# Down tiles that begin wide, wide, narrow, narrow; r copied out of its bank by ScalarE; w_out begun with four column tiles; four other orders of the gates' triples

## The chip, the cores and the metric

The kernel runs on one core of one Trainium2 chip, as one launch. The metric is the device time of an execution in microseconds (us); the lower the better. Before the change three runs took 1267.32, 1267.71 and 1268.02 us, the median is 1267.71.

## The reference

A decoder trunk of two layers on 256 tokens of width 1024, in float32. A layer is a SwiGLU feed-forward (half a step), token mixers in parallel, and a second SwiGLU. Cut to the lines that matter here (`attention` and `gated_linear` stand for the two mixers, which the change doesn't touch):

```python
for l in range(2):
    x = x + 0.5 * swiglu(rmsnorm(x, ffn1_norm[l]), ffn1_w_gate[l], ffn1_w_up[l], ffn1_w_down[l])
    proj = rmsnorm(x, mix_norm[l]) @ w_in[l]             # 1024 -> 6440
    # q_a, kv_a, g_a, q_b, k_b, v_b, a_lr, r_b, g_merge = the column groups of proj
    o_a = attention(q_a, kv_a, sigmoid(g_a))
    o_b = gated_linear(q_b, k_b, v_b, a_lr)
    o_b = rmsnorm(o_b, gla_out_norm[l]) * silu(r_b)
    gm = sigmoid(g_merge)                                # 2 x 1024 columns
    y = gm[0] * (o_a @ w_branch_nsa[l]) + gm[1] * (o_b @ w_branch_gla[l])
    x = x + y @ w_out[l]
    x = x + 0.5 * swiglu(rmsnorm(x, ffn2_norm[l]), ffn2_w_gate[l], ffn2_w_up[l], ffn2_w_down[l])
return rmsnorm(x, final_norm)
# swiglu(x, g, u, d) = (silu(x @ g) * (x @ u)) @ d, with 2816 hidden columns
```

## The kernel before, in words

**Products.** A float32 operand is split into a high part (a cast to float32r) and the low rest. A product is then three matmuls, high by high, high by low, low by high. `mm3` (L120 to L124) issues the three; each is *narrow* (256 columns) or *wide* (512), depending on what streams. `mm2` (L126 to L130) does it in two: a wide one of the weights' high part against [x high | x low] (512 columns), and a narrow one of the weights' low part against x high (256). A pair leaves its two products in the two halves of a bank of PSUM, which are added later. The matmuls of a pair stand at L129 (wide) and L130 (narrow), those of a triple at L122, L123 and L124.

**Weights.** Every weight is read once. A chunk comes from memory by a DMA on SyncE's queue into one of three raw buffers, ScalarE casts it to the high part (L76), and VectorE subtracts to get the low part (L86). `W.prep()` does half a chunk; its calls are written into the program at fixed places, and `W.take()` does what is still missing of the next chunk. Split chunks lie in three buffers.

**The order of the work** is written out by hand: each engine runs its instructions in the order in which the program issues them, and the engines are held together by semaphores. There is no planner.

**FFN** (`ffn`, four times). 22 column tiles of gate and up (`ff`, pairs) make the hidden values h in 22 k-parts; then 8 down tiles `dn` (j = 0 to 7) are made, each from 22 k in two halves of 11 (one chunk each). Tiles 0 to 6 use pairs, tile 7 uses narrow triples (`mmx`, L346), so that only half a bank has to be added at the end. `add_half` (L353) adds 0.5 of the bank to x in two instructions, or in one for j = 7; w_out uses it too (its factor is taken up by the gate). `post_x` then makes x's high and low parts `xh` and `xl` (`split_x`) and the square for the next norm's sum. In the last FFN, `final_x` transposes finished tiles between two halves.

**Mixer** (`mixer`, twice). First come columns in narrow triples, then `block` (L511) eight times: 512 columns for two groups of 128 tokens (tt), with x standing as the weights operand and 512 weight columns streaming, so wide triples, called A (x high by weight high), B (x high by weight low) and C (x low by weight high) in the change. The blocks are v (2), r (2) and the merge gates (n = 0, 1 by e = 0, 1; `gm`). Each block takes two banks of the pool "mm", which has only two, so the next block waits until the last one's banks are read. `slot()` lets the work of attention and of the gated linear mixer in between the matmuls.

For r, ScalarE makes tanh of the bank (`rth`, L539) and VectorE makes (tanh + 1) * bank (`rt`, L541): it is the last reader of the bank. Between them `W.prep()` puts a weight cast and a split.

Then the merge `mg` (wide triples, three chunks for each e) makes y from two branches; gated sums `ym`, `yn` on VectorE (L563, L622) are transposed by PE (`turn`, L569, into `yt`) and split into high and low (`parts`, L576 on ScalarE, L577 on VectorE).

**w_out** makes 8 column tiles `wo` of pairs over 8 k, two to a chunk; the last tile uses triples. The first 4 k are of y's first half (e = 0) and the last 4 k of its second. The first two tiles run interleaved, with the last token group's transposes between them:

```python
for q in range(2):
    for n in range(2):
        for k in range(4 * q, 4 * q + 4):
            self.mm2(bs[n], wh[:, n * NK + k], wl[:, n * NK + k], y[k], k == 0, k == NK - 1)
        if q == 0:
            turn(u[1], 1, yb, (n,))
            parts(ys[n], yb[n], halves[1])
```

Of the kernel before, what the change touches and what calls it, by code (L numbers as in the profile page):

```python
# [9 lines left out]
AF = mybir.ActivationFunctionType  # L10
OP = mybir.AluOpType
# [6 lines left out]
T = 256  # L18
L = 2
FF = 2816  # L20
NK = D // P
NFF = FF // P
# [79 lines left out]
class Trunk:  # L102
# [29 lines left out]
    def mmt(self, b, x, tt, wh, wl, first, last):  # L132

        s = slice(tt * P, tt * P + P)
        self.mm3(b, x[0][:, s], x[1][:, s], wh, wl, first, last)

    def halves(self, o, b):
        self.nc.scalar.activation(o, b[:, T : 2 * T], AF.Copy)  # L138
# [98 lines left out]
    def ffn(self, l, f, next_gain, hook=None):  # L237
        nc, W = self.nc, self.W
        start = l == 0 and f == 0
        hs = []  # L240
        lows = []

        def gate(i, b):

            u = self.t2(f"u{self.uid()}")
            g = u[:, 0:T]
            self.halves(g, b)
            nc.vector.tensor_mul(g, g, self.rbc)  # L248
            nc.scalar.activation(g, g, AF.Silu)  # L249
            return u  # L250

        def gate2(u):
            nc.vector.tensor_mul(u[:, 0:T], u[:, 0:T], self.rbc)

        def up(i, u, b):
            if i % 2 == 0:
                hs.extend(self.splits("h", 2))
            h = u[:, T : 2 * T]
            self.halves(h, b)
            nc.vector.tensor_mul(h, u[:, 0:T], h)  # L260
            nc.scalar.activation(hs[i][0], h, AF.Copy)  # L261
            lows.append((hs[i][1], h, hs[i][0].bitcast(F32)))

        def low():
            nc.vector.tensor_sub(*lows.pop(0))

        wait = None
        for i in range(NFF):
            wh, wl = W.take()
            bs = [self.bank(f"ff{self.uid()}") for _ in range(2)]  # L270
            if i == 0:
                for k in range(NK):
# [24 lines left out]
            W.prep()  # L297
            if not (i == 1 and start):
                gate2(u)
            for k in range(NK):  # L300
                self.mm2(bs[1], wh[:, NK + k], wl[:, NK + k], self.xx[k], k == 0, k == NK - 1)
            if i == 1 and start:
                self.rstd_row()
                u0 = gate(0, wait[0])
                W.prep()
                gate2(u0)
                up(0, u0, wait[1])
                u = gate(i, bs[0])
                W.prep()
                gate2(u)  # L310
                up(i, u, bs[1])
            else:
                up(i, u, bs[1])
                W.prep()
            low()
            if hook:
                hook(i)
        while lows:
            low()
        for j in range(NK):  # L320
            b = self.bank(f"dn{self.uid()}", "mm")
            for half in range(2):
                wh, wl = W.take()
                for r in range(11):
                    k = half * 11 + r
                    self.mmx(j, b, wh[:, r], wl[:, r], hs[k], k == 0, k == NFF - 1)
                if half == 0 or j < NK - 1:
                    W.prep()
                    W.prep()
                if next_gain is None and half == 0 and j > 0:  # L330
                    self.final_x(j - 1)
                    if j == NK - 1:
# [12 lines left out]

    def mmx(self, j, b, lh, ll, x, first, last):  # L346

        if j < NK - 1:
# [4 lines left out]
    def add_half(self, j, b):  # L353
        for s in (slice(0, T), slice(T, 2 * T))[: 2 if j < NK - 1 else 1]:
            self.nc.vector.scalar_tensor_tensor(self.x[j], b[:, s], 0.5, self.x[j], op0=OP.mult, op1=OP.add)  # L355


    def mixer(self, l, next_gain):
# [149 lines left out]
            for i in range(2):  # L508
                T_pair(lambda ps: scaled(t3[:, 2 * i : 2 * i + 2], ps, c))

        def block(evac):  # L511

            bs = [self.bank(f"mm{self.uid()}", "mm") for _ in range(2)]
            for half in range(2):
                wh, wl = W.take()
                for tt in range(2):
                    rest = None
                    for r in range(4):
                        k = half * 4 + r
                        self.mmt(bs[tt], self.xx[k], tt, wh[:, r], wl[:, r], k == 0, k == NK - 1)  # L520
                        if r == 1:
# [13 lines left out]
        def r_evac(n):  # L535

            def go(tt, b):
                th = self.t2(f"rth{self.uid()}")
                nc.scalar.activation(th, b, AF.Tanh, scale=rs2[:, tt : tt + 1])  # L539
# [9 lines left out]
        gm = []  # L549
        for n in range(2):  # L550
            gm.append([self.t4(f"gm{n}{tt}{l}") for tt in range(2)])
            for e in range(2):
                block(lambda tt, b: nc.scalar.activation(
                    gm[n][tt][:, e * 512 : e * 512 + 512], b, AF.Tanh, scale=rs2[:, tt : tt + 1]) and None)
        while gens:
            slot()

# [23 lines left out]
        for e in range(2):  # L581
# [7 lines left out]
            for c in range(3):  # L589
                wh, wl = W.take()  # L590
                for tt in range(2):
                    b = b1[tt] if c else b0[tt]
                    for r in range(4):
                        x = self.oa[r] if c == 0 else self.ob[4 * c - 4 + r]
                        self.mmt(b, x, tt, wh[:, r], wl[:, r], c < 2 and r == 0, c != 1 and r == 3)
                    if c == 0:
                        gated(0, e, tt, b, u[tt])
                    while pending:
# [27 lines left out]
        wh, wl = W.take()  # L626
        bs = [self.bank(f"wo{self.uid()}", "mm") for _ in range(2)]
        for q in range(2):
            for n in range(2):
                for k in range(4 * q, 4 * q + 4):  # L630
                    self.mm2(bs[n], wh[:, n * NK + k], wl[:, n * NK + k], y[k], k == 0, k == NK - 1)
                if q == 0:
                    turn(u[1], 1, yb, (n,))
                    parts(ys[n], yb[n], halves[1])
                else:
                    self.add_half(n, bs[n])
                    W.prep()
                    self.post_x(n, next_gain[:, n : n + 1])
        for i in range(1, 4):
            wh, wl = W.take()  # L640
            for n in range(2):
                j = 2 * i + n
                b = self.bank(f"wo{self.uid()}", "mm")
                for k in range(NK):
                    self.mmx(j, b, wh[:, n * NK + k], wl[:, n * NK + k], y[k], k == 0, k == NK - 1)
                self.add_half(j, b)
                if j < NK - 1:
                    W.prep()
                self.post_x(j, next_gain[:, j : j + 1])
# [670 lines left out]
```

## Time and profile before

| | us |
|---|---|
| median of three runs | 1267.71 |
| lowest, highest | 1267.32, 1268.02 |
| the profiled execution's own time | 1268.17 |
| its span in the trace | 1266.40 |
| PE, DVE, ACT, POOL busy | 1251.6, 913.9, 711.8, 50.5 |

The mean granted clock of TensorE is 0.998 of full speed, and no slice of the span is lower than nine tenths. The profile is of one execution. PE is TensorE's matmuls, PEld its weight loads, DVE VectorE, ACT ScalarE, POOL GpSimd. In a row of the timeline the first number is the start in us from the span's start, the second the busy time of the instruction (or of the group from its first start to its last end), then engine, line, operation, output and inputs, the size, and how many; in brackets the idle time of the engine before it and what ended that. Matmuls are pipelined, so their busy times overlap, and it is the distance from start to start that tells their pace.

### The profile page before, as it was taken

What the parts mean: (1) busy time and instruction counts of PE and PEld (TensorE: products, weight loads), DVE (VectorE), ACT (ScalarE), POOL (GpSimd) and SP (SyncE); (2) the same over time, 40 slices, a digit from 0 to 9 for tenths busy, and PEclk for the clock granted to TensorE, in tenths of its full rate; (3) what the DMA queues carried; (4) which work ended last, traced back from release to release, by engine and by line L of the source; (5) the groups of instructions that cost most, each with busy time, mean ns of one, the idle gap of its engine ahead of it and who ended that gap; (6) DMA issues with size and microseconds to landing.
All of it is one profiled execution on the core that took longest, in us unless ns stands there. A gap on an engine that the chain in (4) does not pass through costs nothing.

```text
span 1266.4 us, 18985 instructions
## 1 busy us (share of the span) xinstructions
PE 1251.6 (99%) x7396; PEld 1076.0 (85%) x7396; DVE 913.9 (72%) x1690; ACT 711.8 (56%) x1265; POOL 50.5 (4%) x60
## 2 busy tenths in 40 slices
PE   9999999999999999999999999999999999999997
PEld 7888889987778888888888888999777788888886
DVE  6888766774755778886578886567656668888753
ACT  5666545566644556655456664456675445566542
POOL 2001101000010000000010000010000100000000
PEclk9999999999999999999999999999999999999999
DMA  7576767334534445545665546573344354555451
GB/s 272 193 230 211 255 201 264 132 124 137 178 118 144 181 168 205 187 154 198 209 224 208 179 150 205 173 283 135 111 156 164 103 199 148 184 200 185 165 190 59
DMA packets 41001, 227.43 MB, mean 180 GB/s; under 512 B 6949, under 2 KB 8109, under 8 KB 21328
## 3 DMA queue, kind: packets, MB, share of 16 engines
q1 hardware_dynamic: 34352, 213.27, 48.7%
q0 software_dynamic: 5840, 11.87, 2.8%
q8 instruction: 58, 0.95, 0.3%
q10 hardware_dynamic: 720, 1.09, 0.3%
q14 instruction: 31, 0.25, 0.1%
HBM read 225.12 MB, written 2.63 MB: 180 GB/s over the span
## 4 chain that ended last, share of the span: by engine, by line
PE 80%; issue 15%; DVE 2%; ACT 2%; DMA 1%; POOL 0%; POOLq 0%; DVEq 0%; ACTq 0%
PE ff L129 19%; PE ff L130 10%; PE dn L129 9%; PE mm L122 7%; PE mm L123 6%; PE mm L124 6%; PE dn L130 4%; PE wo L129 2%; PE mg L122 2%; PE mg L124 2%; PE mg L123 2%; PE O L150 2%; PE o L150 1%; PE s L150 1%; PE wo L130 1%
## 5 line engine op out<-in xcount | busy, mean ns | idle before, releaser
L76 ACT ACTIVATE wh<-raw 128x1024 fp32r<-128x1024 f32 (+3 forms) x445 | 423.4, 967 | 183.6 <-issue 112.3
L86 DVE TENSOR_TENSOR wl<-raw,wh 128x1024 fp32r<-128x1024 f32 (+3 forms) x445 | 491.3, 1119 | 44.0 <-ACT wh L76 43.7
L129 PE MATMUL ff<-xs,wh 128*128 128x512 f32 x1408 | 489.9, 392 | 0.4 <-DVE xs L162 0.4
L130 PE MATMUL ff<-xs,wl 128*128 128x256 f32 x1408 | 393.9, 280 | 0.7 <-DVE wl L1144 0.5
L129 PEld LDWEIGHTS ff<-xs,wh 128*128 128x128 f32 x1408 | 264.4, 188 | 59.2 <-ACT wh L1143 0.8
L130 PEld LDWEIGHTS ff<-xs,wl 128*128 128x128 f32 x1408 | 264.3, 188 | 1.7 <-DVE wl L1144 1.1
L129 PE MATMUL dn<-h,wh 128*128 128x512 f32 x616 | 218.3, 399 | 0.0
L130 PE MATMUL dn<-h,wl 128*128 128x256 f32 x616 | 173.0, 281 | 0.0
L129 PEld LDWEIGHTS dn<-h,wh 128*128 128x128 f32 x616 | 115.7, 188 | 28.3
L139 DVE TENSOR_TENSOR u<-ff,u 128x256 f32<-128x256 f32 x176 | 74.7, 425 | 60.9 <-ACT u L138 60.9
L130 PEld LDWEIGHTS dn<-h,wl 128*128 128x128 f32 x616 | 116.4, 189 | 0.0
L122 PE MATMUL mm<-wh,xs 128*128 128x512 f32 x256 | 106.2, 415 | 2.5 <-DVE rt L541 2.5
L123 PE MATMUL mm<-wl,xs 128*128 128x512 f32 x256 | 101.5, 396 | 0.0
L124 PE MATMUL mm<-wh,xs 128*128 128x512 f32 x256 | 100.9, 394 | 0.0
L249 ACT ACTIVATE u<-u 128x256 f32<-128x256 f32 x88 | 36.8, 419 | 90.8 <-DVE u L248 90.8
L261 ACT ACTIVATE h<-u 128x256 fp32r<-128x256 f32 x88 | 36.8, 418 | 83.9 <-DVE u L260 83.9
L122 PE MATMUL mm<-xs,wh 128*128 128x256 f32 x256 | 73.8, 288 | 0.0
L124 PE MATMUL mm<-xs,wl 128*128 128x256 f32 x256 | 71.7, 280 | 0.0
L123 PE MATMUL mm<-xs,wh 128*128 128x256 f32 x256 | 71.6, 280 | 0.0
L138 ACT ACTIVATE u<-ff 128x256 f32<-128x256 f32 x176 | 65.6, 373 | 9.8 <-PE ff L130 5.4
L355 DVE SCALAR_TENSOR_TENSOR xs<-dn,xs 128x256 f32<-128x256 f32 x60 | 25.5, 424 | 56.0 <-PE dn L130 38.5
L122 PEld LDWEIGHTS mm<-wh,xs 128*128 128x128 f32 x256 | 48.1, 188 | 19.3 <-issue 4.7
(244 smaller groups left out, 1618.1 us busy)
## 6 DMA issues: line engine op xcount, KB each, us to landing
raw<-in_gu SPq DMA_DIRECT2D x85, 1024.0 KB, 4.9
raw<-in_wd SPq DMA_DIRECT2D x64, 704.0 KB, 4.1
raw<-in_wr SPq DMA_DIRECT2D x32, 1024.0 KB, 4.8
raw<-in_wt SPq DMA_DIRECT2D x16, 1024.0 KB, 5.1
raw<-in_wb SPq DMA_DIRECT2D x12, 1024.0 KB, 4.8
w<-in_w POOLq DMA_DIRECT2D x16, 512.0 KB, 8.6
raw<-in_wo SPq DMA_DIRECT2D x8, 1024.0 KB, 4.9
raw<-in_vg SPq DMA_DIRECT2D x4, 592.0 KB, 3.7
```

The source lines that it names most:

```text
L76: self.nc.scalar.activation(wh[:, s], self.raw[c][:, s], AF.Copy)
L86: self.nc.vector.tensor_sub(wl[:, s], self.raw[c][:, s], wh[:, s].bitcast(F32))
L122: mm(out, lh, rh, start=first, stop=False, skip_group_check=True)
L123: mm(out, lh, rl, start=False, stop=False, skip_group_check=True)
L124: mm(out, ll, rh, start=False, stop=last, skip_group_check=True)
L129: mm(b, lh, x[2], start=first, stop=False, skip_group_check=True)
L130: mm(b[:, 0:T], ll, x[0], start=False, stop=last, skip_group_check=True)
L138: self.nc.scalar.activation(o, b[:, T : 2 * T], AF.Copy)
L139: self.nc.vector.tensor_add(o, b[:, 0:T], o)
L150: self.nc.tensor.matmul(out, l, r, start=first, stop=last, skip_group_check=True)
L249: nc.scalar.activation(g, g, AF.Silu)
L261: nc.scalar.activation(hs[i][0], h, AF.Copy)
```

## The change

1. In a half of a down tile (all but the very last half of j = 7) the first two k go through a new function `mm22`: both wide matmuls first, then both narrow ones.
2. The first half of the last down tile uses pairs like the others, and its second half alone triples; the upper half of the bank is added after the first half. The same for w_out's last tile: its first 4 k are pairs.
3. r: ScalarE does the tanh and then copies the bank to `rt`; VectorE computes in place from the copy.
4. The gates' matmuls of two k at a time are issued in another order: for layer 0 n = 0 "A0 C0 B0 A1 C1 B1", layer 0 n = 1 "C0 A0 B0 C1 A1 B1", layer 1 n = 0 "A0 A1 B0 B1 C0 C1", layer 1 n = 1 "A0 B0 A1 B1 C0 C1". The other users of `mmt` (v, r, merge) keep A0 B0 C0 A1 B1 C1.
5. w_out starts with the first 4 k of three tiles, then all four transposes of the last token group, then the fourth tile's first 4 k, then the second halves of the four tiles. Tiles 0 and 1 lie in banks of the pool "sd", tiles 2 and 3 in "mm". One more half of a weight chunk is prepared in the merge, one less after the first tile.

```diff
+    def mm22(self, b, lh, ll, xs, first):
+        mm = self.nc.tensor.matmul
+        for k in range(2):
+            mm(b, lh[:, k], xs[k][2], start=first and k == 0, stop=False, skip_group_check=True)
+        for k in range(2):
+            mm(b[:, 0:T], ll[:, k], xs[k][0], start=False, stop=False, skip_group_check=True)
...
+    def mmt(self, b, xs, tt, wh, wl, first, last, order="A0 B0 C0 A1 B1 C1"):
         s = slice(tt * P, tt * P + P)
-        self.mm3(b, x[0][:, s], x[1][:, s], wh, wl, first, last)
+        ops = order.split()
+        for n, (o, k) in enumerate(ops):
+            k = int(k)
+            self.nc.tensor.matmul(b, xs[k][1 if o == "C" else 0][:, s], wl[:, k] if o == "B" else wh[:, k],
+                                  start=first and n == 0, stop=last and n == len(ops) - 1, skip_group_check=True)
...
                 wh, wl = W.take()
-                for r in range(11):
+                last = j == NK - 1 and half == 1
+                if not last:
+                    self.mm22(b, wh[:, 0:2], wl[:, 0:2], hs[11 * half : 11 * half + 2], half == 0)
+                for r in range(0 if last else 2, 11):
                     k = half * 11 + r
-                    self.mmx(j, b, wh[:, r], wl[:, r], hs[k], k == 0, k == NFF - 1)
+                    self.mmx(last, b, wh[:, r], wl[:, r], hs[k], False, k == NFF - 1)
...
+                if j == NK - 1 and half == 0:
+                    self.add_half(j, b, (1,))
-            self.add_half(j, b)
+            self.add_half(j, b, (0,) if j == NK - 1 else (1, 0))
...
                 nc.scalar.activation(th, b, AF.Tanh, scale=rs2[:, tt : tt + 1])
-                o = rt[tt][:, n * 512 : n * 512 + 512]
-                return lambda: nc.vector.scalar_tensor_tensor(o, th, 1.0, b, op0=OP.add, op1=OP.mult)
+                nc.scalar.activation(o, b, AF.Copy)
+                return lambda: nc.vector.scalar_tensor_tensor(o, th, 1.0, o, op0=OP.add, op1=OP.mult)
...
+                    (("A0 C0 B0 A1 C1 B1", "A0 A1 B0 B1 C0 C1"), ("C0 A0 B0 C1 A1 B1", "A0 B0 A1 B1 C0 C1"))[l][n])
...
                     W.prep()
+                    if e == 1 and c == 0 and tt == 1:
+                        W.prep()
...
+        ws = [W.take() for _ in range(2)]
+        bs = [self.bank(f"wo{self.uid()}", "sd" if j < 2 else "mm") for j in range(4)]
...
+        for j in range(4):
+            out(j, range(4))
+            if j == 2:
+                turn(u[1], 1, yb)
+                for q in range(2):
+                    parts(ys[q], yb[q], halves[1])
+        for j in range(4):
+            out(j, range(4, NK))
+            self.add_half(j, bs[j])
+            if j:
+                W.prep()
+            self.post_x(j, next_gain[:, j : j + 1])
+        for i in range(2, 4):
```

**Where the instructions move: ScalarE at the end of r, layer 0.** `rth` is the tanh of a bank `mm`, `wh` a weight cast, `gc`, `ga` and `ge` are side work of the gated linear mixer, `gm` the first gate. Before:

```order
L539 ACTIVATE rth_3370<-mm_3310,rs_112_2100 128x512
L76 ACTIVATE wh_3345<-raw_3254 128x1024
L774 ACTIVATE gc_3334<-gb_3263 128x512
L775 ACTIVATE ga_3262<-gb_3263 128x512
L780 ACTIVATE ge_3335<-ge_3335 128x512
L539 ACTIVATE rth_3394<-mm_3311,rs_112_2100 128x512
L76 ACTIVATE wh_3396<-raw_3305 128x1024 x2
```

After:

```order
L560 ACTIVATE rth_3362<-mm_3302,rs_112_2090 128x512
L561 ACTIVATE rt_2402<-mm_3302 128x512
L76 ACTIVATE wh_3337<-raw_3244 128x1024
L808 ACTIVATE gc_3326<-gb_3253 128x512
L809 ACTIVATE ga_3252<-gb_3253 128x512
L814 ACTIVATE ge_3327<-ge_3327 128x512
L560 ACTIVATE rth_3387<-mm_3303,rs_112_2090 128x512
L561 ACTIVATE rt_2403<-mm_3303 128x512
L76 ACTIVATE wh_3390<-raw_3297 128x1024 x2
```

A copy of 128x512 stands behind each tanh, ahead of the weight cast; the third and fourth tanh of a layer have two and three such copies in front of them, counting those of the first block. The rest keeps its order.

**VectorE at the start of w_out, layer 0.** `xs<-wo` is the addition of a tile's bank to x (two instructions), `wl` a weight split, `xs_90` to `xs_92` the low parts `xl` of tiles 0 to 2, `sq` the sum of squares, `y<-yt` the split of y. Before:

```order
L86 TENSOR_TENSOR wl_4050<-raw_3969,wh_4049 128x1024
L577 TENSOR_TENSOR y_3979<-yt_4067,y_3979 128x2x128
L577 TENSOR_TENSOR y_3980<-yt_4068,y_3980 128x2x128
L355 SCALAR_TENSOR_TENSOR xs<-wo_4103,xs 128x256 x2
L86 TENSOR_TENSOR wl_4098<-raw_4021,wh_4097 128x1024
L162 SCALAR_TENSOR_TENSOR xs_90<-xs,sm,xs_90 128x256
L355 SCALAR_TENSOR_TENSOR xs<-wo_4104,xs 128x256 x2
L86 TENSOR_TENSOR wl_4098<-raw_4021,wh_4097 128x1024
L162 SCALAR_TENSOR_TENSOR xs_91<-xs,sm,xs_91 128x256
L175 TENSOR_TENSOR sq_4143<-sq_4143,sq_4163 128x256
L355 SCALAR_TENSOR_TENSOR xs<-wo_4166,xs 128x256 x2
```

After:

```order
L86 TENSOR_TENSOR wl_4068<-raw_4015,wh_4067 128x1024
L599 TENSOR_TENSOR y_3973<-yt_4063,y_3973 128x2x128
L599 TENSOR_TENSOR y_3974<-yt_4064,y_3974 128x2x128
L375 SCALAR_TENSOR_TENSOR xs<-wo_4099,xs 128x256 x2
L175 SCALAR_TENSOR_TENSOR xs_90<-xs,sm,xs_90 128x256
L375 SCALAR_TENSOR_TENSOR xs<-wo_4100,xs 128x256 x2
L86 TENSOR_TENSOR wl_4068<-raw_4015,wh_4067 128x1024
L175 SCALAR_TENSOR_TENSOR xs_91<-xs,sm,xs_91 128x256
L188 TENSOR_TENSOR sq_4155<-sq_4155,sq_4175 128x256
L375 SCALAR_TENSOR_TENSOR xs<-wo_4101,xs 128x256 x2
L86 TENSOR_TENSOR wl_4168<-raw_4035,wh_4167 128x1024
```

The split between the first tile's addition and its `xl` is gone from there; one half chunk is split earlier, in front of the `y` steps (the chunk after the two that w_out's first four tiles use). The third addition, of wo_4101 (j = 2), now frees a bank that the fifth tile takes.

**PE at the start of a down tile.** `h` are two k of the hidden values, each row one matmul of one k. Before:

```order
L129 MATMUL dn_1423<-h_12_304,wh_1300 128x512
L130 MATMUL dn_1423<-h_12_304,wl_1301 128x256
L129 MATMUL dn_1423<-h_12_304,wh_1300 128x512
L130 MATMUL dn_1423<-h_12_304,wl_1301 128x256
L129 MATMUL dn_1423<-h_17_368,wh_1300 128x512
```

After (a row with x2 is two matmuls in a row):

```order
L136 MATMUL dn84_1423<-h0_12_304,wh22_1300 128x512 x2
L138 MATMUL dn84_1423<-h0_12_304,wl22_1301 128x256 x2
L129 MATMUL dn84_1423<-h0_17_368,wh22_1300 128x512
L130 MATMUL dn84_1423<-h0_17_368,wl22_1301 128x256
L129 MATMUL dn84_1423<-h0_17_368,wh22_1300 128x512
```

The second wide matmul has moved ahead of the first narrow one; from the third k on nothing moves.

## Rows read from the trace of the kernel before

**Rows 1.** The page's first part: busy time, share of the span and instructions of each engine.

```profile
span 1266.4 us, 18985 instructions
PE 1251.6 (99%) x7396; PEld 1076.0 (85%) x7396; DVE 913.9 (72%) x1690; ACT 711.8 (56%) x1265; POOL 50.5 (4%) x60
```

**Rows 2.** The waits of PE: engine, line and tile that waited, what it waited for, then us in total, times, longest.

```profile
PE mm L122 <- DVE rt L541: 2.5, 2, 1.2
...
PE yt L569 <- DVE ym L622: 0.8, 2, 0.4
...
PE wo L129 <- DVE y L577: 0.4, 2, 0.2
PE ff L130 <- DVE wl L86: 0.2, 1, 0.2
```

**Rows 3.** Timeline of ACT at the end of the r blocks of layer 0, with the row of the next gap.

```profile
325.15 0.67 ACT L539 ACTIVATE rth<-mm,rs 128x512 f32<-128x512 f32 x1
325.72 1.04 ACT L76 ACTIVATE wh<-raw 128x1024 fp32r<-128x1024 f32 x1
...
328.30 0.67 ACT L539 ACTIVATE rth<-mm,rs 128x512 f32<-128x512 f32 x1
328.87 2.00 ACT L76 ACTIVATE wh<-raw 128x1024 fp32r<-128x1024 f32 x2
333.36 1.06 ACT L76 ACTIVATE wh<-raw 128x1024 fp32r<-128x1024 f32 x1 [2.49 <-issue]
```

**Rows 4.** Timeline of PE at the end of r and the start of the first gate block, layer 0: the last matmul on r's first bank and the first one of the gate block there, then around the second bank.

```profile
325.56 0.39 PE L124 MATMUL mm<-wh,xs 128*128 128x512 f32 x1
327.18 0.50 PE L122 MATMUL mm<-wh,xs 128*128 128x512 f32 x1 [1.23 <-DVE rt L541]
...
329.86 0.39 PE L124 MATMUL mm<-wh,xs 128*128 128x512 f32 x1
330.20 0.50 PE L122 MATMUL mm<-wh,xs 128*128 128x512 f32 x1
```

**Rows 5.** Timeline of DVE in the same stretch: the two steps `rt`, and the weight split between them.

```profile
326.44 0.68 DVE L541 SCALAR_TENSOR_TENSOR rt<-rth,mm 128x512 f32<-128x512 f32 x1
...
328.33 1.22 DVE L86 TENSOR_TENSOR wl<-raw,wh 128x1024 fp32r<-128x1024 f32 x1
329.47 0.68 DVE L541 SCALAR_TENSOR_TENSOR rt<-rth,mm 128x512 f32<-128x512 f32 x1
```

**Rows 6.** Timeline of ACT at an unscaled copy of a 128x512 bank (L809), with the instruction behind it.

```profile
342.51 0.60 ACT L809 ACTIVATE kst<-tb 128x512 f32<-128x512 f32 x1 [1.03 <-PE tb L808]
343.00 1.05 ACT L76 ACTIVATE wh<-raw 128x1024 fp32r<-128x1024 f32 x1
```

**Rows 7.** Timeline of PE in a block of the mixer: two rows with one wide triple between them.

```profile
315.06 0.39 PE L124 MATMUL mm<-wh,xs 128*128 128x512 f32 x1
...
315.76 0.39 PE L124 MATMUL mm<-wh,xs 128*128 128x512 f32 x1
```

**Rows 8.** Timeline of PE in w_out of layer 0: its first matmul, the matmuls ahead of and behind the two pairs of transposes, the first matmul of the third tile (431.27), and the first one behind w_out (448.28).

```profile
423.96 0.48 PE L129 MATMUL wo<-y,wh 128*128 128x512 f32 x1
...
425.34 0.28 PE L130 MATMUL wo<-y,wl 128*128 128x256 f32 x1
426.04 0.44 PE L569 MATMUL yt<-cst,ym 128*128 128x128 f32 x2 [0.42 <-DVE ym L622]
...
427.73 0.38 PE L569 MATMUL yt<-cst,ym 128*128 128x128 f32 x2
428.30 0.50 PE L129 MATMUL wo<-y,wh 128*128 128x512 f32 x1 [0.19 <-DVE y L577]
...
431.27 0.40 PE L129 MATMUL wo<-y,wh 128*128 128x512 f32 x1
...
448.28 0.39 PE L129 MATMUL ff<-xs,wh 128*128 128x512 f32 x1
```

**Rows 9.** Timeline of DVE in w_out of layer 0: the last step of `ym`, and the additions of the first three tiles with the split and `xl` of the first.

```profile
426.35 0.43 DVE L622 TENSOR_TENSOR ym<-ym,yn 128x256 f32<-128x256 f32 x1
...
430.05 0.88 DVE L355 SCALAR_TENSOR_TENSOR xs<-wo,xs 128x256 f32<-128x256 f32 x2 [1.07 <-PE wo L130]
...
432.38 0.88 DVE L355 SCALAR_TENSOR_TENSOR xs<-wo,xs 128x256 f32<-128x256 f32 x2
...
435.04 0.88 DVE L355 SCALAR_TENSOR_TENSOR xs<-wo,xs 128x256 f32<-128x256 f32 x2
```

**Rows 10.** Timeline of ACT in the same place: the step `xh` of the first tile.

```profile
430.97 0.51 ACT L161 ACTIVATE xs<-xs,sm 128x256 fp32r<-128x256 f32 x1 [1.49 <-DVE xs L355]
```

**Rows 11.** Timeline of PE in the last down tile of the first FFN: narrow triples.

```profile
194.00 0.28 PE L122 MATMUL dn<-h,wh 128*128 128x256 f32 x1
194.12 0.28 PE L123 MATMUL dn<-h,wh 128*128 128x256 f32 x1
194.24 0.28 PE L124 MATMUL dn<-h,wl 128*128 128x256 f32 x1
194.36 0.28 PE L122 MATMUL dn<-h,wh 128*128 128x256 f32 x1
```

**Rows 12.** Timeline of PE in an earlier down tile of the first FFN: the first row and the row three pairs later.

```profile
150.09 0.40 PE L129 MATMUL dn<-h,wh 128*128 128x512 f32 x1
...
151.15 0.40 PE L129 MATMUL dn<-h,wh 128*128 128x512 f32 x1
```

**Rows 13.** The same in a down tile of the last FFN, behind transposes of `final_x`.

```profile
1214.41 0.39 PE L129 MATMUL dn<-h,wh 128*128 128x512 f32 x1
...
1215.45 0.39 PE L129 MATMUL dn<-h,wh 128*128 128x512 f32 x1
```

**Rows 14.** Timeline of PE in the merge: two rows with one wide triple between them.

```profile
404.28 0.39 PE L122 MATMUL mg<-wh,ob 128*128 128x512 f32 x1
...
404.96 0.39 PE L122 MATMUL mg<-wh,ob 128*128 128x512 f32 x1
```

More of the change, by code (lines that the diff above doesn't have):

```diff
@@ L130, in mm2 @@
         mm(b[:, 0:T], ll, x[0], start=False, stop=last, skip_group_check=True)
-    def mmt(self, b, x, tt, wh, wl, first, last):
-        s = slice(tt * P, tt * P + P)
-        self.mm3(b, x[0][:, s], x[1][:, s], wh, wl, first, last)
+    def mm22(self, b, lh, ll, xs, first):
[5 more added lines that the diff above has]
+    def mmt(self, b, xs, tt, wh, wl, first, last, order="A0 B0 C0 A1 B1 C1"):
+        s = slice(tt * P, tt * P + P)
+        ops = order.split()
[3 more added lines that the diff above has]
+                                  start=first and n == 0, stop=last and n == len(ops) - 1, skip_group_check=True)
     def halves(self, o, b):
@@ L344, in ffn, with mmx @@
         W.prep()
-    def mmx(self, j, b, lh, ll, x, first, last):
-        if j < NK - 1:
+    def mmx(self, tail, b, lh, ll, x, first, last):
+        if not tail:
             self.mm2(b, lh, ll, x, first, last)
@@ L351, in mmx, with add_half @@
             self.mm3(b[:, 0:T], lh, ll, x[0], x[1], first, last)
-    def add_half(self, j, b):
-        for s in (slice(0, T), slice(T, 2 * T))[: 2 if j < NK - 1 else 1]:
+    def add_half(self, j, b, parts=(1, 0)):
+        for p in parts:
+            s = slice(p * T, p * T + T)
             self.nc.vector.scalar_tensor_tensor(self.x[j], b[:, s], 0.5, self.x[j], op0=OP.mult, op1=OP.add)
@@ L509, in mixer, with block @@
                 T_pair(lambda ps: scaled(t3[:, 2 * i : 2 * i + 2], ps, c))
-        def block(evac):
+        def block(evac, order="A0 B0 C0 A1 B1 C1"):
             bs = [self.bank(f"mm{self.uid()}", "mm") for _ in range(2)]
@@ L517, in block @@
                     rest = None
-                    for r in range(4):
+                    for r in (0, 2):
                         k = half * 4 + r
-                        self.mmt(bs[tt], self.xx[k], tt, wh[:, r], wl[:, r], k == 0, k == NK - 1)
-                        if r == 1:
+                        self.mmt(bs[tt], self.xx[k : k + 2], tt, wh[:, r : r + 2], wl[:, r : r + 2], k == 0, k == NK - 2, order)
+                        if r == 0:
                             slot()
@@ L538, in go @@
                 th = self.t2(f"rth{self.uid()}")
+                o = rt[tt][:, n * 512 : n * 512 + 512]
                 nc.scalar.activation(th, b, AF.Tanh, scale=rs2[:, tt : tt + 1])
-                o = rt[tt][:, n * 512 : n * 512 + 512]
-                return lambda: nc.vector.scalar_tensor_tensor(o, th, 1.0, b, op0=OP.add, op1=OP.mult)
+                nc.scalar.activation(o, b, AF.Copy)
+                return lambda: nc.vector.scalar_tensor_tensor(o, th, 1.0, o, op0=OP.add, op1=OP.mult)
             return go
@@ L553, in mixer @@
                 block(lambda tt, b: nc.scalar.activation(
-                    gm[n][tt][:, e * 512 : e * 512 + 512], b, AF.Tanh, scale=rs2[:, tt : tt + 1]) and None)
+                    gm[n][tt][:, e * 512 : e * 512 + 512], b, AF.Tanh, scale=rs2[:, tt : tt + 1]) and None,
+                    (("A0 C0 B0 A1 C1 B1", "A0 A1 B0 B1 C0 C1"), ("C0 A0 B0 C1 A1 B1", "A0 B0 A1 B1 C0 C1"))[l][n])
         while gens:
@@ L592, in mixer @@
                     b = b1[tt] if c else b0[tt]
-                    for r in range(4):
-                        x = self.oa[r] if c == 0 else self.ob[4 * c - 4 + r]
-                        self.mmt(b, x, tt, wh[:, r], wl[:, r], c < 2 and r == 0, c != 1 and r == 3)
+                    xs = self.oa if c == 0 else self.ob[4 * c - 4 : 4 * c]
+                    for r in (0, 2):
+                        self.mmt(b, xs[r : r + 2], tt, wh[:, r : r + 2], wl[:, r : r + 2], c < 2 and r == 0, c != 1 and r == 2)
                     if c == 0:
@@ L623, in mixer, with out @@
                     W.prep()
[L626 to L639, printed above, removed]
+                    if e == 1 and c == 0 and tt == 1:
+                        W.prep()
+        ws = [W.take() for _ in range(2)]
+        bs = [self.bank(f"wo{self.uid()}", "sd" if j < 2 else "mm") for j in range(4)]
+        def out(j, ks):
+            wh, wl = ws[j // 2]
+            for k in ks:
+                r = j % 2 * NK + k
+                self.mm2(bs[j], wh[:, r], wl[:, r], y[k], k == 0, k == NK - 1)
+        for j in range(4):
[11 more added lines that the diff above has]
+        for i in range(2, 4):
             wh, wl = W.take()
@@ L644, in mixer @@
                 for k in range(NK):
-                    self.mmx(j, b, wh[:, n * NK + k], wl[:, n * NK + k], y[k], k == 0, k == NK - 1)
-                self.add_half(j, b)
+                    self.mmx(j == NK - 1 and k > 3, b, wh[:, n * NK + k], wl[:, n * NK + k], y[k], k == 0, k == NK - 1)
+                    if j == NK - 1 and k == 3:
+                        self.add_half(j, b, (1,))
+                self.add_half(j, b, (0,) if j == NK - 1 else (1, 0))
                 if j < NK - 1:
```

## The prediction, made before the changed kernel ran

> **What bounds the kernel now.** I read the share of busy time first, then the waits of TensorE, then the starts of its matmuls in five places, and last the other engines beside the places that the change touches. TensorE (PE) is busy 99% of a span of 1266.40 us [rows 1]. So the time is the sum of the distances between matmul starts, and another engine counts only where PE waits for it. In the two mixers PE waits twice for the r gate's VectorE step (`rt`), twice for `ym` and twice for `y` before w_out [rows 2]; two times is once per layer, so I work out layer 0 and double it.
>
> All sums are made against the profiled execution's own 1268.17 us (1.77 outside the span); it is 0.46 above the median 1267.71 of the three timed runs, so the forecast is moved down by 0.46 at the end. A measurement of this kernel can tell about 0.2%, 2.5 us, from no change.
>
> **r, copied out of its bank.** ScalarE (ACT) now does tanh and copy, and VectorE works from the copy, so that the bank is free after the copy and no longer after VectorE. In the stretch from 325.15 to 330.87 ACT has no gap [rows 3]: whatever is put in moves all that follows, up to the gap of 2.49 at 333.36, which takes it in. PE's last r matmul of the first bank starts at 325.56, its next one at 327.18, where the beat would be 0.23: 1.39 lost; at the second bank 329.86 to 330.20 loses 0.11 [rows 4]. Both are ended by the VectorE step: it starts 326.44 and 329.47 and takes 0.68, so it ends 327.12 and 330.15 [rows 5].
>
> What a copy costs ACT: the only unscaled copy of a 128x512 bank in the trace takes 0.60, and the next instruction starts 0.49 after it [rows 6]; with a scale operand, as the tanh has, the next starts 0.57 after [rows 3]. I take 0.50, by the row that is alike; the ends are 0.49 and 0.69 (nothing overlaps). Two copies (for the first two tanh) precede the third tanh, which starts at 325.15 + 1.00 = 326.15; its copy runs from 326.72 to 327.32. PE gets the first bank at 327.32 in place of 327.12: +0.20. The fourth tanh has three copies before it: 328.30 + 1.50 = 329.80, its copy 330.37 to 330.97: the second bank is late by 0.82 against 330.15. PE, itself 0.20 late, would be there at 330.09 + 0.20, before the bank is free; so the delays don't add, and the larger one stays. **+0.82 per layer, +1.64 in all.** Bounds: with 0.69 per copy and no overlap the fourth pair starts at 328.30 + 3 x 0.69 = 330.37 and ends 0.67 + 0.60 later, 331.64: +1.5 per layer (+3.0); if the waits simply went, -1.50 per layer (-3.0). The weights' casts stand behind the copies: the gates' second chunk has its last split at 328.33 to 329.55 [rows 5], would have it by about 331, and PE comes to it 8 triples of 0.70 [rows 7] after 327.18, at 332.8. That distance hides it; without it the excess would be seen in full, and PE's waits know only one of 0.2 for such a split [rows 2].
>
> The Trainium skill ("ScalarE: Activation LUTs", What ACT_TABLE_LOAD costs) gives an activation 186 ns + 0.833 ns per element, 93 ns more for each pointer operand, with 93 ns of overlap back to back. That makes an estimate of 0.52 for the copy where the row has 0.49, and +0.88 per layer for +0.82; the row is used.
>
> **w_out.** Before, the first 16 pairs are interrupted twice, each time by two transposes: 425.34 to 426.04 ahead of the first, 427.73 to 428.30 behind the second; the 16 pairs end at 431.27, 7.31 after 423.96, where 16 x 0.3533 = 5.65 is the beat alone. The rest runs without a wait to 448.28, 24.32 in all [rows 8]. After, three tiles' first four k stand ahead of the transposes: 12 x 0.3533 + 0.08 for the first start = 4.32, until 428.28. VectorE ended the last `ym` at 426.78 before [rows 9]; even with a step or two moved ahead of it, it is there by 428.28. The transposes take 0.35 and no wait; j = 3 begins at 428.64 and ends its half at 430.13; the second halves follow, j = 0 until 431.55. So far 1.1 us is gained.
>
> What is late next: the additions that free the banks. Before, the first tile's addition starts at 430.05, the second tile's at 432.38, the third's at 435.04 [rows 9]; now four tiles are held at once, in two "sd" and two "mm" banks, and the fifth tile needs the bank of j = 2. The first addition starts about 0.2 after j = 0 ends, at 431.76. In the new order no weight split stands between it and the step `xl`, but `xl` waits for ACT's `xh`, which starts 0.92 after the addition and takes 0.51 [rows 10]; it starts at +1.43 and the second addition at +1.86. From there to the third there is the step of 2.66 seen before (432.38 to 435.04: addition, split, `xl`, `sq`) [rows 9], so +4.52, and its two parts take 0.88: the bank is free at 431.76 + 5.40 = 437.16, PE starts at 437.22. PE's fourth tile ends at 431.55 + 3 x 1.413 = 435.80. A new wait of 1.42. Later tiles don't wait, since PE needs 8 x 0.3533 = 2.83 for a tile and VectorE 2.66. PE in all: 60 pairs x 0.3533 + 4 triples x 0.36 = 22.64, transposes 0.35, wait 1.42, three restarts of 0.085 = 0.26: 24.67 for 24.32. **+0.36 per layer, +0.72 in all.** Bounds: without the bank wait -1.07 per layer; with 0.6 more at the transposes +0.96. Behind w_out the last `xl` is needed at the eighth k of the next FFN's first tiles, 14 pairs of 0.347 = 4.9 after their start, and follows the last addition by three steps of about 0.5: it stays hidden.
>
> **The last down tile.** Its first half goes as 11 pairs (353.3 ns) where it had 11 triples of 360 (three narrow ones at 120, [rows 11]): 44 x 6.7 ns over four FFNs = **-0.29**. The six more additions on VectorE (0.42 each) stand where it waits for PE. Bounds: 0 and -0.6 (at 346.7).
>
> **Down halves begin wide, wide, narrow, narrow.** Pairs of down tiles run at two beats with the same shapes: 1.06 us for three pairs, 353.3 each [rows 12], in all tiles but two of the last FFN, where three take 1.04, 346.7 [rows 13]. Which beat holds is set by the start of the stretch, not by an operand. The new start has wide after wide, 0.68 for three = 226.7 in the merge [rows 14], and narrow after narrow, 120 [rows 11]: 346.7 between them; I put the two mixed steps at the fast 346.7 as well, so 693.3 for 706.7, -13.3 ns for each of 60 halves: **-0.80**. The other nine pairs of a half I leave at the slow beat, which returned after every ordinary start. Ends: 0, and the fast beat for all: 60 x 9 x 6.67 ns = -3.6 more.
>
> The Trainium skill ("TensorE: Matmul & The Clock Gate", Back-to-back issue gap) gives an isolated matmul N/2.4 + 2.5 ns, set by columns alone. By it a pair has one price, 325 ns, in any order, and the down term would be 0. The rows show 353.3 and 346.7 for one and the same pair, so the measurement decides.
>
> **The gates' orders.** 128 wide triples (2 layers, 2 n, 2 e, 16) stand at 0.70 each [rows 7], and I cost four other orders of them at **0**: the operands are the same, and the merge shows that triples in the old order can run at 0.68 too. Ends: -20 ns x 128 = -2.6 if the 226.7 beat comes, and +2.6 if it is a step of 20 ns worse.
>
> **Sum.** 1.64 + 0.72 - 0.29 - 0.80 + 0 = +1.27; 1268.17 + 1.27 - 0.46 = 1269.0.
>
> **Rivals.** (A) The down tiles take the fast beat throughout: 3.6 less, 1265.4. For it: the fast beat exists [rows 13] and began after a disturbed start. Against: it came in two of six such tiles. (B) The waits go and nothing takes their place: r -3.0 for +1.64, w_out -2.1 for +0.72, so 1269.0 - 7.5 = 1261.5. For it: the shape of both edits. Against: ACT without a gap [rows 3], and the bank of j = 2. (C) Slower: the gates' orders put two accumulating matmuls on the same weights or the same x further apart or closer, and their beat falls one step, 20 ns a triple: +2.6, 1271.6. It decides from two of four orders on (1270.3, where slower begins). For it: 233.3 against 226.7 shows that wide matmuls have several beats; against: the extra time of 0.70 showed in no fixed place of the triple. (D) The same with the 226.7 beat: 1266.4.
>
> **Chances.** Forecast 0.48 (its own range 1267.8 to 1270.4), A 0.22, B 0.09, C 0.13, D 0.08. A lies at the bound of 1265.2, so half of it and what meets with D is faster: faster 0.11 + 0.04 + 0.09 = 0.24 and some 0.02 of down tiles beyond; slower is C with the copies' price at its end, 0.13 + 0.11 = 0.24; same 0.50. The range takes in A and most of C: 1264.9 to 1271.3.
>
> **What the profile would show.** Right: PE waits for the fourth `rt` copy on ACT, not for VectorE, about 0.8 longer in r; PE has no wait at the transposes of w_out and one of 1.4 us at its fifth tile, for VectorE's addition; pairs of down tiles at 1.06 per three after the first four matmuls. Wrong: no idle of PE in r (B), three pairs in 1.04 in most down tiles (A), gate triples off 0.70 (C, D).

## The result, and the profile after

The changed kernel takes 1280.74 us (median of four runs, 1279.12 to 1282.64) where the kernel before takes 1267.63: a ratio of 1.0103, 95% interval 1.0088 to 1.0118. It is 13.1 us slower, and far outside the forecast range of 1264.9 to 1271.3. The profiled execution is the fastest of the four, 1279.12 with a span of 1277.4. The four runs lie further apart than those of the kernel before (3.5 us for 0.7), and their granted clocks differ, 0.994 in the slowest and 0.997 in the fastest.

The page's first part hardly differs from [rows 1]; PE is busy for the same time, and the span is 11 us longer, so PE waits:

```profile
span 1277.4 us, 18901 instructions
PE 1251.1 (98%) x7344; PEld 1073.8 (84%) x7344; DVE 916.1 (72%) x1696; ACT 715.1 (56%) x1273; POOL 49.8 (4%) x60
```

The waits of PE after, to be read beside [rows 2] (columns as there):

```profile
PE wo L122 <- DVE xs L375: 5.4, 2, 2.8
PE dn L122 <- DVE xs L375: 3.8, 3, 1.3
PE mm L147 <- ACT rt L561: 3.8, 4, 1.4
PE wo L129 <- DVE xs L375: 2.7, 2, 1.3
```

The third and fourth line were forecast: r now waits for ScalarE's copy, and w_out's fifth tile for a bank. The first two were not. L122 is the first matmul of a triple; triples stand in the second part of the last down tile and of w_out's last tile, and L375 is the addition of a bank to x. PE waits there 9.2 us in all.

Where it is lost by stage, from windows cut at the first matmul of each stage (its length; then PE's busy time and number, its granted clock, the DMA share and GB/s). Of the kernel before: the down tiles of the first FFN, the wide blocks of layer 0, w_out of layer 0 and of layer 1.

```profile
134.20:196.52 62.32, 62.32 (x376) 1.00 0.65 221
267.75:389.96 122.21, 120.88 (x588) 1.00 0.40 138
423.96:448.28 24.32, 23.71 (x143) 1.00 0.46 157
1046.25:1070.57 24.32, 23.71 (x144) 1.00 0.46 156
```

The same four of the changed kernel:

```profile
133.86:196.98 63.12, 61.87 (x366) 1.00 0.62 222
268.20:391.13 122.93, 120.96 (x589) 1.00 0.39 137
425.12:453.92 28.80, 24.68 (x140) 0.95 0.41 146
1054.33:1081.92 27.59, 23.65 (x140) 1.00 0.43 153
```

So +0.80 in the down tiles (the second and third FFN show the same), +0.72 in the wide blocks of layer 0 (+0.69 in layer 1), +4.48 and +3.27 in the two w_outs; the down stage of the last FFN is 0.4 shorter. That makes the 11 us between the two traces; the other 2 us between the medians stand in no trace. The forecast had about -0.3 for each down stage, +0.82 and +0.36.

**The wait that was not forecast.** PE at the last down tile of the first FFN:

```profile
191.42 0.28 PE L130 MATMUL dn<-h,wl 128*128 128x256 f32 x1
192.95 0.35 PE L122 MATMUL dn<-h,wh 128*128 128x256 f32 x1 [1.25 <-DVE xs L375]
```

VectorE at that time, the splits of two half chunks, the early addition and, at 197.18, the addition of the lower half:

```profile
190.12 2.35 DVE L86 TENSOR_TENSOR wl<-raw,wh 128x1024 fp32r<-128x1024 f32 x2
192.39 0.42 DVE L375 SCALAR_TENSOR_TENSOR xs<-dn,xs 128x256 f32<-128x256 f32 x1
197.18 0.42 DVE L375 SCALAR_TENSOR_TENSOR xs<-dn,xs 128x256 f32<-128x256 f32 x1 [4.38 <-PE dn L124]
```

A narrow matmul is followed by the next one after 0.12, so the triples could have started at 191.54. They start at 192.95, when the addition of the *upper* half of the bank has ended (192.39 + 0.42 = 192.81), although they write only the lower half. The early addition waits neither for PE nor for data: it stands behind the two splits in VectorE's order.

In w_out of layer 0 VectorE is a whole tile behind, and the same wait is longer. PE, then VectorE:

```profile
448.13 0.28 PE L130 MATMUL wo<-y,wl 128*128 128x256 f32 x1
451.19 0.58 PE L122 MATMUL wo<-y,wh 128*128 128x256 f32 x1 [2.78 <-DVE xs L375]
```

```profile
448.06 0.88 DVE L375 SCALAR_TENSOR_TENSOR xs<-wo,xs 128x256 f32<-128x256 f32 x2
448.85 1.21 DVE L86 TENSOR_TENSOR wl<-raw,wh 128x1024 fp32r<-128x1024 f32 x1
...
450.72 0.42 DVE L375 SCALAR_TENSOR_TENSOR xs<-wo,xs 128x256 f32<-128x256 f32 x1
```

The tile before it is added at 448.06, then come a split, `xl` and `sq`, and only at 450.72 the half bank for which PE waits. The clock follows in this layer; windows of PE around it, columns as above:

```profile
448.20:451.20 3.00, 0.22 (x3) 0.95 0.90 303
451.20:453.92 2.72, 2.72 (x13) 0.50 0.12 51
453.92:457.00 3.08, 3.08 (x18) 0.94 0.02 5
```

The 12 matmuls of the four triples run at a granted clock of 0.50, the lower level of 1.2 GHz, and take 2.72. In layer 1 PE waited 2.60, the clock stayed at 1.00, and the same 12 take 1.53 (1080.39 to 1081.92): that is the 1.2 us by which w_out of layer 0 is longer. The spread of the four runs and of their clocks would fit such falls, in one place or in more; no trace shows it.

### The profile page after: what moved, and what is told of

It is laid out like the page before. It is cut to its first block, busy times and chain, and to the rows that moved or that the text cites. A ratio compares the mean times of both kernels' runs of the same rounds, so it can differ in the third digit from the quotient of the medians.

```text
span 1277.4 us, 18901 instructions
## 1 busy us (share of the span) xinstructions
PE 1251.1 (98%) x7344; PEld 1073.8 (84%) x7344; DVE 916.1 (72%) x1696; ACT 715.1 (56%) x1273; POOL 49.8 (4%) x60
## 5 line engine op out<-in xcount | busy, mean ns | idle before, releaser
L129 PE MATMUL dn<-h,wh 128*128 128x512 f32 x540 | 191.6, 396 | 0.0
L147 PE MATMUL mm<-wh,xs 128*128 128x512 f32 x512 | 170.9, 405 | 3.8 <-ACT rt L561 3.8
L130 PE MATMUL dn<-h,wl 128*128 128x256 f32 x540 | 150.6, 279 | 0.0
L147 PEld LDWEIGHTS mm<-wh,xs 128*128 128x128 f32 x512 | 94.2, 188 | 31.1 <-ACT rt L561 5.5
L129 PEld LDWEIGHTS dn<-h,wh 128*128 128x128 f32 x540 | 101.4, 188 | 21.4
L130 PEld LDWEIGHTS dn<-h,wl 128*128 128x128 f32 x540 | 101.8, 188 | 0.0
L147 PE MATMUL mm<-wl,xs 128*128 128x512 f32 x256 | 98.9, 396 | 0.0
L122 PE MATMUL mm<-xs,wh 128*128 128x256 f32 x256 | 73.8, 288 | 0.0
L375 DVE SCALAR_TENSOR_TENSOR xs<-dn,xs 128x256 f32<-128x256 f32 x64 | 27.1, 424 | 56.6 <-PE dn L130 38.1
L147 PEld LDWEIGHTS mm<-wl,xs 128*128 128x128 f32 x256 | 48.2, 188 | 9.9
```

The source lines that it names most:

```text
L122: mm(out, lh, rh, start=first, stop=False, skip_group_check=True)
L147: self.nc.tensor.matmul(b, xs[k][1 if o == "C" else 0][:, s], wl[:, k] if o == "B" else wh[:, k], start=first and n == 0, stop=last and n ...
```

## The experiments

All ratios are against the kernel before, run on the same chip.

**The addition moved behind the triples.**

```diff
-                if j == NK - 1 and half == 0:
-                    self.add_half(j, b, (1,))
-            self.add_half(j, b, (0,) if j == NK - 1 else (1, 0))
+            self.add_half(j, b)
...
-                    if j == NK - 1 and k == 3:
-                        self.add_half(j, b, (1,))
-                self.add_half(j, b, (0,) if j == NK - 1 else (1, 0))
+                self.add_half(j, b)
```

> The changed kernel, but the upper half of the last tile's bank (down and w_out) is added behind the triples, together with the lower half. Theory 1 (the triples wait because VectorE has still to read the other half of the same bank): PE's waits of L122 for the addition, 5.4 us in w_out and 3.8 us in the down tiles, go, and with them the lower clock behind the first of them: about 1270. Theory 2 (VectorE is behind there whatever it has to add, and the triples wait for other work of its queue, such as a weight split): the waits stay under another name, 1278 to 1281.

Measured: 1267.84, ratio 1.0001 (0.9992 to 1.0010). Both waits of L122 are gone, and with them the whole difference from the kernel before (that the rest of the change comes out near nothing is a cancellation, see below). The last pair and the first triple of the same tile:

```profile
191.24 0.28 PE L130 MATMUL dn<-h,wl 128*128 128x256 f32 x1
191.36 0.28 PE L122 MATMUL dn<-h,wh 128*128 128x256 f32 x1
```

0.12 apart, while VectorE is in the same two splits (189.94 to 192.29 here). Theory 2 falls: the splits' results are not what the triples wait for.

**The early addition kept, the triples in a bank of their own.**

```diff
+                    if last and r == 0:
+                        b = self.bank(f"dn{self.uid()}")
-                    self.mmx(last, b, wh[:, r], wl[:, r], hs[k], False, k == NFF - 1)
+                    self.mmx(last, b, wh[:, r], wl[:, r], hs[k], last and r == 0, k == NFF - 1)
...
-                    self.add_half(j, b, (1,))
+                    self.add_half(j, b)
```

(and the same at k = 4 of w_out's last tile)

> The changed kernel with the early addition kept, but the last tile's triples go into a bank of their own, so that three additions are made in place of two. Theory 1 (same bank): no wait of PE at L122, about 1270, like the late addition. Theory 2 (a late VectorE holds PE whatever bank it reads): a wait of 1.2 us at each down tile and 2.6 to 2.8 us at each w_out stays, 1278 to 1281.

Measured: 1267.44, ratio 0.9998 (0.9989 to 1.0007). The addition stands where it stood, and PE doesn't wait:

```profile
192.11 0.28 PE L130 MATMUL dn<-h,wl 128*128 128x256 f32 x1
192.23 0.28 PE L122 MATMUL dn<-h,wh 128*128 128x256 f32 x1
```

It is the shared bank, shown from both sides. The Trainium skill has the rule ("PSUM — Partial Sum Buffer", PSUM bank collisions raise a hardware error): two engines must not touch one bank in the same partitions at the same time, other columns of it included, so a program has to guard PSUM by bank and not by address. The waits agree with it, 1.25 us in the down tile and 2.78 in w_out, both for columns that PE didn't write; what a collision itself does no run here shows. Nor do the two edits tell the bank from the tile that the program lays over the whole of it: the second moves the triples to another tile as well as to another bank.

**Wide, wide, narrow, narrow alone, in every half of tiles 0 to 6.** The kernel before with `mm22` and:

```diff
+                kick = j < NK - 1
+                if kick:
+                    self.mm22(b, wh[:, 0:2], wl[:, 0:2], hs[11 * half : 11 * half + 2], half == 0)
-                for r in range(11):
+                for r in range(2 if kick else 0, 11):
```

> The kernel before with only this added: every half of down tiles 0 to 6 begins wide, wide, narrow, narrow. Theory 1 (each such start turns the beat over, slow to fast and fast to slow, so that every second half is fast): 56 halves by about -0.04 us = -2.3, 1265.3. Theory 2 (the forecast: the beat falls back to slow behind it): 56 halves by -0.013 = -0.75, 1266.9. Theory 3 (the fast beat in all halves came with something else in the change): no difference, 1267.6.

Measured: 1266.07, ratio 0.9984 (0.9975 to 0.9993); the down stage of the first FFN goes from 62.32 to 61.77, 0.55 for 14 halves, 0.039 each. Theory 1 had 0.04. In the changed kernel the alternation can be read. A half at the slow beat, three pairs, and behind the next start a half at the fast beat, three pairs:

```profile
155.17 0.40 PE L129 MATMUL dn<-h,wh 128*128 128x512 f32 x1
...
156.23 0.40 PE L129 MATMUL dn<-h,wh 128*128 128x512 f32 x1
...
157.64 0.40 PE L129 MATMUL dn<-h,wh 128*128 128x512 f32 x1
...
158.68 0.39 PE L129 MATMUL dn<-h,wh 128*128 128x512 f32 x1
```

1.06 and 1.04, as in [rows 12] and [rows 13].

**One such start for each FFN.** In place of `j < NK - 1`:

```diff
+                kick = j == 0 and half == 0
```

> The kernel before with one such start for each FFN, at the first half of down tile 0 alone. Theory 1 (the start turns the beat over, and it then stays): 14 halves of three FFNs fast, 42 by -0.07 us = -2.9, and a little of the last FFN, whose transposes start the beat anew: about 1264.5. Theory 2 (the beat falls back to slow): 4 by -0.013, no difference, 1267.6.

Measured: 1264.78, ratio 0.9977 (0.9968 to 0.9986). Fewer starts gain more, which only theory 1 allows: the down stage of the first FFN takes 61.30, -1.02 for -0.55, and far behind the single start the beat is still the fast one, three pairs in 1.03:

```profile
170.12 0.39 PE L129 MATMUL dn<-h,wh 128*128 128x512 f32 x1
...
171.15 0.40 PE L129 MATMUL dn<-h,wh 128*128 128x512 f32 x1
```

**r's copies alone.** The kernel before with the edit of `r_evac` and nothing else.

```diff
                 nc.scalar.activation(th, b, AF.Tanh, scale=rs2[:, tt : tt + 1])
...
+                nc.scalar.activation(o, b, AF.Copy)
-                return lambda: nc.vector.scalar_tensor_tensor(o, th, 1.0, b, op0=OP.add, op1=OP.mult)
+                return lambda: nc.vector.scalar_tensor_tensor(o, th, 1.0, o, op0=OP.add, op1=OP.mult)
```

> The kernel before with the copies of r's banks on ScalarE alone. Theory 1 (three copies stand ahead of the fourth one's end on a ScalarE without a gap): PE waits 0.7 us longer in r of each layer, as in the changed kernel: +1.4, 1269.2. Theory 2 (the copies cost nothing by themselves, and the 0.7 is the gates' orders): no difference, 1267.8, and PE waits 2.5 us for r as before.

Measured: 1269.30 against 1267.80, ratio 1.0011 (1.0002 to 1.0020): +1.5, by theory 1. The wait has changed its name and grown from 2.5:

```profile
PE mm L122 <- ACT rt L541: 3.8, 4, 1.4
```

**The gates' orders alone.** The kernel before with the new `mmt` and the four orders.

```diff
+                    (("A0 C0 B0 A1 C1 B1", "A0 A1 B0 B1 C0 C1"), ("C0 A0 B0 C1 A1 B1", "A0 B0 A1 B1 C0 C1"))[l][n])
```

> The kernel before with the four orders of the gates' matmuls alone. Theory 1 (a wide matmul's pace doesn't hang on the order): the stage of wide blocks within 0.05 us of 122.22, 1267.8 in all. Theory 2 (the orders cost the 0.7 us): the stage 122.9, 1269.2.

Measured: 1267.71 against 1267.80, ratio 1.0000 (0.9991 to 1.0009); the stage of wide blocks takes 122.22 in layer 0, as before. The orders change neither.

**w_out's start alone, with the banks exchanged.** r, gates, down tiles and last tile as before; the line that differs from the changed kernel's start:

```diff
-        bs = [self.bank(f"wo{self.uid()}", "sd" if j < 2 else "mm") for j in range(4)]
+        bs = [self.bank(f"wo{self.uid()}", "mm" if j < 2 else "sd") for j in range(4)]
```

> The kernel before with w_out's four-tile start alone, and tiles 0 and 1 in the banks of pool mm, 2 and 3 in those of sd (the changed kernel has it the other way round); the last tile all in triples. Theory 1 (PE's wait of 1.34 at the fifth tile is for the bank of tile 2, and the bank of tile 0 is free long before): no wait there, w_out 24.3 - 1.1 = 23.2 in each layer, -2.2 in all, 1265.6. Theory 2 (VectorE is behind, and PE meets it a tile or two later): the wait moves and w_out stays at 24.3 to 24.5.

Measured: 1268.13, ratio 1.0002 (0.9993 to 1.0011), w_out 24.42 in layer 0. Theory 1 falls. The fifth tile doesn't wait any more, the seventh does, for the bank of the fifth; PE's row, then VectorE's:

```profile
442.43 0.47 PE L129 MATMUL wo<-y,wh 128*128 128x512 f32 x1 [0.99 <-DVE xs L371]
```

```profile
441.41 0.88 DVE L371 SCALAR_TENSOR_TENSOR xs<-wo,xs 128x256 f32<-128x256 f32 x2
```

The four tiles' second halves end 1.41 apart, and VectorE needs 2.66 for each tile, so it falls behind there by more than a bank can hold.

**What paid, put together, and r's second block in other banks.** One start for each FFN, the triples in banks of their own, w_out as in the run before, r and gates as before the change, and:

```diff
-            block(r_evac(n))
+            block(r_evac(n), "sd" if n else "mm")
```

(`block` takes its two banks from that pool)

> What paid or should pay together: one wide, wide, narrow, narrow start for each FFN; w_out's four-tile start with tiles 0 and 1 in the banks of mm; the last tiles' first halves in pairs and their triples in a bank of their own; r without copies, as before, but the second r block in two banks of pool sd, so that the gates' first block needn't wait for it. If r's wait of 1.5 us a layer goes without a new one: 1267.8 - 3.0 (beat) - 2.2 (w_out) - 3.0 (r) - 0.5 = 1259. If attention's side work, which uses the same pool, waits for those banks instead: 1262 or more, with a new wait of PE in the r or gate blocks.

Measured: 1260.90, ratio 0.9944 (0.9932 to 0.9957). r's wait is gone: the wide blocks take 120.48 in layer 0, 1.73 less than before, without a new one. w_out keeps its wait of 0.99, so its 2.2 of the expected sum are missing.

**w_out's last two tiles in pool sd too.**

```diff
-                b = self.bank(f"wo{self.uid()}", "mm")
+                b = self.bank(f"wo{self.uid()}", "mm" if i == 2 else "sd")
```

> The best version so far with the last two tiles of w_out in banks of pool sd as well, so that no tile of w_out takes a bank whose addition is still behind. Theory 1 (the wait of 0.99 us in each layer is for a bank only): it goes, and the next FFN starts 1.0 earlier: -2.0, 1258.9. Theory 2 (VectorE itself is behind, and what it owes at the end, the last low part of x, holds the next FFN's first tile): PE waits there instead, for xl or for a weight split, and the time stays at 1260.5 to 1260.9.

Measured: 1259.07, ratio 0.9933 (0.9919 to 0.9946). Theory 1: w_out takes 23.17 in both layers, 1.15 less than before. The gate and up stage behind each w_out is 0.18 longer, a remnant of theory 2: in layer 0 its fifteenth pair starts at 449.08 in place of 449.01, and its narrow matmul 0.34 behind the wide one where the others need 0.23. The pair is the first to need the last `xl`, which ends at 449.02. PE's rows, then VectorE's:

```profile
448.89 0.28 PE L130 MATMUL ff<-xs,wl 128*128 128x256 f32 x1
449.08 0.51 PE L129 MATMUL ff<-xs,wh 128*128 128x512 f32 x1
```

```profile
448.54 0.48 DVE L175 SCALAR_TENSOR_TENSOR xs<-xs,sm,xs 128x256 fp32r<-128x256 f32 x1 [0.58 <-ACT xs L174]
```

The longest waits of PE that are left stand at the start and the end of the program and at the norm:

```profile
PE wb L163 <- DVE mhalf L1176: 1.5, 1, 1.5
PE ff L129 <- DVE xs L175: 1.2, 1, 1.2
PE stl L163 <- ACT sq L182: 1.0, 1, 1.0
PE st L163 <- DVE acc L1223: 0.5, 1, 0.5
```

**The start in every half of the last FFN as well.**

```diff
-                kick = half == 0 and j == 0
+                kick = j == 0 and half == 0 or next_gain is None and not last
```

> The same with, in the last FFN alone, the wide, wide, narrow, narrow start in every half, since transposes start the beat anew there. If a start turns the beat over from where the transposes left it, most halves there are fast, as in the changed kernel: last FFN's down stage about 0.4 to 0.5 us shorter, 1258.4 with theory 1. If not: no difference to the run before.

Measured: 1258.83, ratio 0.9931 (0.9919 to 0.9944). The last FFN's stage is 0.65 shorter in the trace; between the two medians 0.24 is less than their runs are apart, so the time doesn't tell them apart. Either beats both kernels: 8.5 to 8.8 us under the one before, some 22 under the changed one.

## Why the prediction was wrong

**The step that failed** is one sentence in the part on the last down tile: "The six more additions on VectorE (0.42 each) stand where it waits for PE", with bounds of 0 and -0.6. It priced the additions as work of VectorE and found cover for that. It did not ask who is queued behind them: PE's triples, by the bank. VectorE does wait for PE in that tile, 4.38 us, but only behind the early addition; where the addition could have started, two splits of 2.35 in all (or in w_out a tile's backlog) stand in front of it. So a wait was added that the working has no term for: 3.8 us in the down tiles, 5.4 in w_out, and about 1.2 of slow clock behind one of them. Removing that wait alone, by either edit, brings the time back to 1267.4 to 1267.8, where the forecast, which had no term for the wait, had 1269.0. What is left of the change nearly cancels: the down tiles gain, r and w_out lose. Most of the 1.2 to 1.6 us under the forecast is the down tiles, where each of the first three FFNs gains 0.70 with the late addition (62.32 to 61.62) and the forecast's two terms make 0.27.

**The other terms, by the trace.**

- r: forecast +0.82 per layer, measured +0.72 and +0.69. The third tanh starts at 326.57, which is 326.12 with the 0.45 by which the stage began later taken off, for 326.15 forecast. The copies:

```profile
326.57 0.67 ACT L560 ACTIVATE rth<-mm,rs 128x512 f32<-128x512 f32 x1
327.14 0.58 ACT L561 ACTIVATE rt<-mm 128x512 f32<-128x512 f32 x1
327.62 1.06 ACT L76 ACTIVATE wh<-raw 128x1024 fp32r<-128x1024 f32 x1
```

 The copy is 0.58 long, and the next instruction starts 0.48 behind its start; [rows 6] had 0.60 and 0.49. The estimate of 0.52 that the prediction worked out from the Trainium skill ("ScalarE: Activation LUTs", What ACT_TABLE_LOAD costs) is 0.04 above the 0.48 of the row; the r term hardly feels it.
- w_out: forecast +0.36 per layer with a wait of 1.42 at the fifth tile. The wait is there, 1.34 long in both layers, for the third tile's addition; PE's transposes wait for nothing. Without the failed step the stage takes 24.54 for 24.32, +0.22; 0.08 of the difference is the shorter wait.

```profile
436.84 0.28 PE L130 MATMUL wo<-y,wl 128*128 128x256 f32 x1
438.46 0.47 PE L129 MATMUL wo<-y,wh 128*128 128x512 f32 x1 [1.34 <-DVE xs L375]
```

- The last down tile's first half, as pairs with the new start: forecast -0.08 per FFN, measured -0.15 with the late addition (61.62 for the 61.77 of the run with the starts alone). That is near the end of -0.6 in all that the prediction gave for the fast beat.
- Down halves: forecast -0.013 each, measured -0.039. The mechanism behind the number was half right: the fast beat does come with the start, but the start *turns* the beat over, so it comes in every second half. Rival A (fast throughout) fell for the same reason; with one start for each FFN it holds in the first three, whose down stages take 61.30 each. An isolated price by columns alone, as the Trainium skill gives it ("TensorE: Matmul & The Clock Gate", Back-to-back issue gap), would have made both experiments on the start equal to the kernel before; they are 1.7 and 3.0 us under it.
- The gates: forecast 0, measured 0. Rivals C and D fell.
- Rival B had the wait in w_out simply go. It fell in the form that the change has and in the one with exchanged banks; it holds with banks enough for VectorE's backlog, and for r with the second block in other banks (1.73 less in layer 0).

The chances for "slower" (0.24) rested on the gates and the copies, not on what made it slower.

## What to carry to other kernels

An instruction that is moved forward is priced by who waits for its end as well as by its own time: here an early read of half a bank held the later writes into that bank until the reader's queue had come to it. Give the later writes a bank of their own, or read late. Where the busiest engine waits for a bank, first count the banks that another engine's backlog needs; exchanging two of them only moved the wait, two more removed it. And before a start is written into every tile to reach a better beat, try it once.

## What the runs showed of the hardware that was not expected

- Two steady beats of one and the same stream of matmul pairs, 353.3 and 346.7 ns, between which a single start of wide, wide, narrow, narrow moves it, in either direction; a beat once set holds for 13 halves on end (61.30 us for a stage of 62.32).
- After a wait of 2.78 us PE's granted clock fell to 0.50 for the next 2.72 us in one layer, and after one of 2.60 in the other layer it stayed at 1.00.
- Four orders of wide triples, with x's and the weights' parts repeated at other distances, run at the same pace (the stage takes 122.22 us in layer 0 and 122.19 in layer 1, for 122.22 and 122.23 before).
